# Taking the narrow weight blocks of a two-layer decoder eight or four at a time instead of two

## The chip, the cores and the metric

The kernel runs on one core of a Trainium2 chip. The metric is the device time of one execution in microseconds (us). A core has five engines that run side by side and wait for each other through semaphores: TensorE (PE, matrix products into PSUM; PEld is the part of it that loads the stationary operand), VectorE (DVE), ScalarE (ACT), GpSimd (POOL) and SyncE (SP, which here only issues transfers). Sixteen DMA engines move data between HBM and the core's memory.

## The reference, cut to what matters

A decoder trunk of two layers, width 2048, on 256 tokens, all in fp32. Both layers end in the same squared-ReLU MLP, which holds most of the weights.

```
def squared_relu_mlp(h, w1, w2):
    z = jax.nn.relu(h @ w1)          # w1: 2048 x 8192
    return (z * z) @ w2              # w2: 8192 x 2048

for i in range(2):
    if i == 1:
        sk1, sk2, sv = shared_kv(x, kv_norm, w_kv, k_norm, cos, sin)
    u = rms_norm(x, mix_norm[i]) @ w_in[i]          # 2048 x 2048
    # layer 0: causal pooling mixer; layer 1: differential attention; both: memory attention
    x = x + concat([token_out, mem_out]) @ w_out[i] # 2048 x 2048
    x = x + squared_relu_mlp(rms_norm(x, ffn_norm[i]), w_ff1[i], w_ff2[i])
```

## The kernel before

**Numbers in two parts.** Each fp32 operand is held as a high part, rounded to the TensorE format fp32r, and a low part, the rest. A product is high times high, plus high times low, plus low times high. The activations of 128 features lie side by side as 256 columns of high parts and 256 columns of low parts, 512 columns in all.

**Narrow and wide.** The weights come in blocks of 128 x 128, laid out in HBM in the order of use, eight to a row of 128 x 1024. In a *narrow* product one block is the stationary operand and the activations stream past it. The block's high part meets all 512 columns; its low part meets only the 256 high columns and adds to the second half of the same PSUM bank. So a block costs one matmul of 512 columns and one of 256, each with its own weight load. Narrow products are:

- the up projection `w_ff1` of each MLP: `up_tile` calls `narrow` (L940) with 16 blocks, 64 tiles a layer;
- the rest of the down projection `w_ff2`: `down_tile` calls `narrow` with 20 blocks, 8 tiles a layer;
- the output projection `w_out` and the pooling part of `w_in`: `a_part` (L512), whose tiles have 16 blocks, some of them in pieces.

In a *wide* product the activations are stationary and four blocks (a quad, 512 columns of weights) stream past: `wide_step`, `b_tile`, and the slab jobs of the MLP (`run`, L1038 to L1040), which work off most of `w_ff2` by a scheme of seven products in place of eight. A third form, `c_tile` (L533 to L538) and `group_w` (L1345 to L1347), uses a block with three matmuls of 256 columns.

**Pairs.** Both narrow loops take two blocks at a time: two high matmuls, then two low ones (L522 and L524 in `a_part`, L947 and L949 in `narrow`). After every four blocks they call `tick()`.

**The feed.** Class `Feed` hands out the blocks. For each job ACT rounds a piece of a loaded row into the high ring (L178) and DVE subtracts to make the low part (L181). In the MLP's up projection a job is a whole row, eight blocks (`rows_whole`, kept in `plan.whole`); elsewhere it is a quad. `fill` prepares three jobs ahead, when the first block of a job is asked for; `used` gives the slots back at the end of a row or quad. The ring has six slots of a quad, with two more in the MLP (`slot`).

**Deferred work.** `at(d, fn)` puts a piece of work d ticks ahead; `tick` runs what is due. The ReLU, squares and splits of the MLP (`convert`, at up to 10 ticks behind a tile) and the collecting of finished banks are placed so.

**Order.** The code is written in one order; a scheduler under it then orders each engine's instructions by its own estimate of times, so that small changes in the code can swap neighbours on ACT, DVE and SP. In the MLP up tiles and slab jobs alternate by `ffn_plan`: as a rule an up tile, then two or four slab jobs. While the seven slab banks are open, all up tiles share one PSUM bank, `x_bank`: ACT copies it out (L961) before the next tile may start.

Of the kernel before, what the change touches and what calls it, by code (L numbers as in the profile page):

```python
# [19 lines left out]
T = 256  # L20
# [85 lines left out]
class Feed:  # L106
# [151 lines left out]
    def block(self, what):  # L258
# [2 lines left out]
        s = slice(self.pos % 4 * P, self.pos % 4 * P + P)  # L261
        return hi[:, s], lo[:, s]

    def used(self, n=1):
        self.pos += n
        if self.dry:
            self.plan.npos = self.pos
        elif (self.pos - 1) // 8 in self.plan.whole:
            if self.pos % 8 == 0:
                self.free(("R", self.pos // 8 - 1))  # L270
        elif self.pos % 4 == 0:
            self.free(("N", self.pos // 4 - 1))
# [91 lines left out]
def program(ctx, tc, plan, dry, xT, memT, par, lam, cst, wst, yT):  # L364
    nc = tc.nc
# [9 lines left out]
    feed = Feed(tc, wst, wp, tp, plan, dry)  # L375
# [10 lines left out]
    def tick():  # L386
        now[0] += 1
        for _, fn in sorted(pend.pop(now[0], []), key=lambda r: r[0]):
            fn()
# [9 lines left out]
    def bk(tag, name, shape=(P, 512)):  # L399
        return pp.tile(list(shape), F32, tag=tag, bufs=1, name=name)  # L400
# [3 lines left out]
    def mmt(name):  # L404
        turnm[0] += 1
        return bk(f"m{(turnm[0] - 1) % 3}", name)
# [7 lines left out]
    def in_halves(name):  # L414
        return Halves(
            [sp.tile([P, NK // 2, 512], F32R, tag=f"S2{i}", name=f"{name}{i}") for i in "ab"]
        )
# [94 lines left out]
    def a_part(ps, w, l, n, ks, xs, first=True, last=True):  # L512
        ks = list(ks)
        i = 0
        while i < len(ks):
            two = []
            for k in ks[i : i + (1 if feed.pos % 2 else 2)]:
                two.append((i, k, *feed.block((w, l, k, n, 1))))
                feed.used()
                i += 1  # L520
            for j, k, hi, lo in two:
                nc.tensor.matmul(ps, hi, xs[:, k, :], start=first and j == 0, stop=False)  # L522
            for j, k, hi, lo in two:
                nc.tensor.matmul(  # L524
                    ps[:, T : 2 * T], lo, xs[:, k, 0:T], start=False,
                    stop=last and j == len(ks) - 1,
                )
            if feed.pos % 4 == 0:
                tick()

    def c_tile(ps, w, l, n, ks, xs):
# [306 lines left out]
    def ffn(l, xs, tag, done):  # L838
# [99 lines left out]
                at(d, fn)  # L938

        def narrow(ps, w, n, ks, src):  # L940
            for j in range(0, len(ks), 2):
                two = []
                for k in ks[j : j + 2]:
                    two.append((k, *feed.block((w, l, k, n, 1))))
                    feed.used()
                for k, hi, lo in two:
                    nc.tensor.matmul(ps, hi, src(k), start=k == ks[0], stop=False)  # L947
                for k, hi, lo in two:
                    nc.tensor.matmul(  # L949
                        ps[:, T : 2 * T], lo, src(k)[:, 0:T], start=False, stop=k == ks[-1]  # L950
                    )
                if j % 4 == 2:
                    tick()

        def up_tile(j, ps):
            narrow(ps, "w_ff1", j, list(range(NK)), lambda k: xs[:, k, :])
            if j == 1:
                r2c.append(columns("x")[1])
                r2.append(rstd_from("x"))
                nc.scalar.activation(r2[0], r2[0], AF.Square)  # L960
            nc.scalar.copy(pairs[j // 2 % 3][:, 512 * (j % 2) : 512 * (j % 2) + 512], ps)  # L961
            if j % 2:
                convert(j // 2, (1, 1, 2, 2, 3, 4, 5, 6) if j == 63 else STEPS)
# [7 lines left out]
        def down_tile(q, n, ps):  # L971
            ks = list(range(2 * NB, 4 * NK))
            if l == 1 and q == 3 and n == 7:
                narrow(ps, "w_ff2", n, ks[:-4], z)
                end = mmt("end")
                nc.scalar.copy(douts[downs[0] % 2], ps)
                add_down(n, douts[downs[0] % 2])
                for k in ks[-4:]:
                    hi, lo = feed.block(("w_ff2", l, k, n, 1))
                    zk = z(k)  # L980
                    nc.tensor.matmul(end[:, 0:T], hi, zk[:, 0:T], start=k == ks[-4], stop=False)
                    nc.tensor.matmul(end[:, 0:T], hi, zk[:, T : 2 * T], start=False, stop=False)
                    nc.tensor.matmul(end[:, 0:T], lo, zk[:, 0:T], start=False, stop=k == ks[-1])
                    feed.used()
                tick()
                for i in range(NB, 32):
                    left(i, "N")
                rest = douts[(downs[0] + 1) % 2][:, 0:T]
                nc.vector.tensor_mul(rest, end[:, 0:T], r2[0])
                nc.vector.tensor_add(resid[:, n, :], resid[:, n, :], rest)  # L990
                done(n)
                return
            narrow(ps, "w_ff2", n, ks, z)
            for i in range(NB, 32):
                left(i, "N")
# [206 lines left out]
    xs = in_halves("xs0")  # L1202
# [75 lines left out]
    ps = [mmt("mq0"), bk("o", "mq0")]  # L1278
# [28 lines left out]
    def group_u(g):  # L1307
        up = ups[g % 2]
        for c in range(3):
            ps = mmt("u")  # L1310
            a_part(ps, "w_in", 0, 3 * g + c, range(NK), xs)
            low = vt("u_c")
            nc.scalar.copy(low, ps[:, T : 2 * T])
            nc.vector.tensor_add(low, ps[:, 0:T], low)
            nc.vector.tensor_mul(up[:, c, 16:], low, x_r[0])
# [37 lines left out]
    def out_tiles(l, cat, lead, ks, fx, between):  # L1353

        first = [mmt("wo") for _ in range(3)]
        for i, part in enumerate(lead):
            for n in range(3):
                a_part(first[n], "w_out", l, n, part, cat, first=i == 0, last=False)
        between()
        for n in range(NK):  # L1360
            if n < 3:
                ps = first[n]
                a_part(ps, "w_out", l, n, ks, cat, first=False)
            else:
                ps = bk(f"n{n - 3}", "wo") if n < 5 else mmt("wo")
                a_part(ps, "w_out", l, n, sum(lead, []) + ks, cat)
            resid_add(ps, n)
            resid_done(n, [(fx, G_FFN + 16 * l)])
# [86 lines left out]
    def pair_of_banks(c, name):  # L1455
        if c % 2:
            return [bk(f"n{i}", name) for i in range(2)]
        return [mmt(name) for _ in range(2)]

    for c in range(3):  # L1460
        ps = pair_of_banks(c, "k1") if c else [mmt("k1"), bk("o", "k1")]
# [8 lines left out]
    for c in range(3):  # L1470
        ps = pair_of_banks(c + 1, "v1")
# [183 lines left out]
    for c in range(3):  # L1655
        ps = pair_of_banks(0, "q1")
# [4 lines left out]
        for i in range(2):  # L1661
            j = 2 * c + i
# [10 lines left out]
    for h in range(4):  # L1673
        ps = bk((ma, mb, mc, mb)[h], "mq1")
# [16 lines left out]
    for n, part in parts + [(n, range(NK)) for n in range(5, NK)]:  # L1691
        first = n not in opened
# [12 lines left out]
    down, _ = ffn(1, fx1, "S1", lambda n: nc.sync.dma_start(yT[:, n, :], resid[:, n, :]))  # L1705
# [84 lines left out]
```

## Time and profile before

| | |
|---|---|
| median of 3 runs | 2014.07 us (2012.58 to 2014.2) |
| the profiled execution's own time | 2016.58 us |
| its span | 2014.8 us |
| DVE busy | 1754.6 us (87%) |
| ACT busy | 1371.6 us (68%) |
| POOL busy | 163.3 us (8%) |
| HBM read, written | 425.61 MB, 12.58 MB |
| granted TensorE clock | 1.0 throughout |

The span runs from the first instruction to the last; 1.8 us of the execution lie around it. Busy times count a matmul from its start to its modelled end, and matmuls overlap, so PE's busy share does not say how fast it works; the starts in the timeline do. An engine's idle time counts only where it is waited for.

### The profile page before, as it was taken

Reading aid. Unit: us, or ns where it says so; the run is one execution under the profiler, and the core shown is the slowest. Engines: PE = TensorE matmul, PEld = TensorE weight load, DVE = VectorE, ACT = ScalarE, POOL = GpSimd, SP = SyncE. Lnnn points to the kernel's source line nnn. Section 1 sums busy time; section 2 is a strip of 40 time slices with the busy share of each in tenths; the row PEclk is TensorE's granted clock in tenths of the full one; section 3 lists DMA queues with packets and bytes.
Section 4 is the critical chain, followed back from the end, with each engine's and each line's share of the span. In section 5 each row is a group of like instructions: output and inputs, shape, how many; then the busy total and the mean of one; then the engine's idle time right before and its main releaser. Section 6 shows DMA issues by size and latency. Waiting matters only on the chain.

```text
span 2014.8 us, 30584 instructions
## 1 busy us (share of the span) xinstructions
PE 2003.7 (99%) x10636; PEld 1709.2 (85%) x10636; DVE 1754.6 (87%) x2665; ACT 1371.6 (68%) x2209; POOL 163.3 (8%) x191
## 2 busy tenths in 40 slices
PE   9999999999999999999999999999999999999999
PEld 7888888888888888888888889888888888888887
DVE  8888778999999999998775698878899999999987
ACT  7765467676666677667665698557676677677664
POOL 0001300000001110000000000320000000101000
PEclk9999999999999999999999999999999999999999
DMA  9566767777878888756656545666777877878775
GB/s 310 183 195 201 231 205 214 239 226 227 247 230 241 250 224 264 214 180 214 227 183 195 187 143 174 216 222 213 234 233 221 247 223 231 264 232 240 243 214 157
DMA packets 135370, 442.95 MB, mean 220 GB/s; under 512 B 15344, under 2 KB 18416, under 8 KB 135216
## 3 DMA queue, kind: packets, MB, share of 16 engines
q1 hardware_dynamic: 117216, 406.39, 60.4%
q0 software_dynamic: 17856, 34.61, 10.4%
q8 instruction: 83, 1.36, 0.3%
q14 instruction: 71, 0.58, 0.1%
q10 hardware_dynamic: 144, 0.01, 0.0%
HBM read 425.61 MB, written 12.58 MB: 217 GB/s over the span
## 4 chain that ended last, share of the span: by engine, by line
PE 55%; DVE 1%; DMA 1%; ACT 1%; issue 0%; POOL 0%; ACTq 0%; DVEq 0%; POOLq 0%
PE x_bank L947 13%; PE x_bank L949 6%; PE p L1038 5%; PE p L1040 5%; PE p L1039 5%; PE wo L522 3%; PE k L553 3%; PE v L553 3%; PE q L553 3%; PE ff L947 2%; PE wo L524 1%; PE mv L553 1%; PE mk L553 1%; PE ff L949 1%; DMA c_b<-part 1%; DVE lo_ring L181 1%
## 5 line engine op out<-in xcount | busy, mean ns | idle before, releaser
L181 DVE TENSOR_TENSOR lo_ring<-raw,hi_ring 128x512 fp32r<-128x512 f32 (+1 forms) x685 | 570.1, 847 | 128.4 <-ACT hi_ring L178 121.3
L178 ACT CAST hi_ring<-raw 128x512 fp32r<-128x512 f32 (+1 forms) x685 | 497.5, 741 | 231.4 <-PE wo L522 67.2
L181 DVE TENSOR_TENSOR lo_ring<-slab,hi_ring 128x1024 fp32r<-128x1024 f32 (+1 forms) x324 | 334.5, 1042 | 48.9 <-ACT hi_ring L178 47.3
L178 ACT CAST hi_ring<-slab 128x1024 fp32r<-128x1024 f32 (+1 forms) x324 | 293.5, 907 | 112.9 <-DVE slab L212 56.9
L149 POOL DMA_DIRECT2D slab<-in_w x108 | 93.6, 867 | 1575.9 <-DVE lo_ring L181 468.8
L947 PE MATMUL x_bank<-fx,hi_ring 128*128 128x512 f32 x664 | 209.2, 395 | 0.0
L522 PE MATMUL wo<-cat,hi_ring 128*128 128x512 f32 x512 | 161.6, 396 | 0.0
L178 ACT CAST slot<-slab 128x1024 fp32r<-128x1024 f32 x108 | 113.4, 1050 | 68.0 <-PE x_bank L947 62.8
L181 DVE TENSOR_TENSOR slot<-slab,slot 128x1024 fp32r<-128x1024 f32 x108 | 131.8, 1220 | 21.7 <-ACT slot L178 21.2
L949 PEld LDWEIGHTS x_bank<-fx,lo_ring 128*128 128x128 f32 x664 | 124.7, 188 | 29.4
L947 PE MATMUL x_bank<-fx0b,hi_ring 128*128 128x512 f32 x472 | 148.2, 395 | 0.0
L961 ACT COPY room<-x_bank 128x512 f32<-128x512 f32 x118 | 68.9, 584 | 99.2 <-PE x_bank L949 99.1
L212 DVE TENSOR_TENSOR slab<-slab,slab 128x1024 f32<-128x1024 f32 x108 | 131.6, 1218 | 0.4
L949 PE MATMUL x_bank<-fx,lo_ring 128*128 128x256 f32 x664 | 130.8, 278 | 0.0
L524 PEld LDWEIGHTS wo<-cat,lo_ring 128*128 128x128 f32 x512 | 96.0, 188 | 22.0
L949 PEld LDWEIGHTS x_bank<-fx0b,lo_ring 128*128 128x128 f32 x472 | 88.7, 188 | 21.0
L947 PEld LDWEIGHTS x_bank<-fx,hi_ring 128*128 128x128 f32 x664 | 103.0, 189 | 2.2
L524 PE MATMUL wo<-cat,lo_ring 128*128 128x256 f32 x512 | 101.7, 278 | 0.0
L178 ACT CAST slot<-raw 128x1024 fp32r<-128x1024 f32 (+1 forms) x76 | 74.1, 976 | 28.6 <-PE x_bank L947 21.9
L181 DVE TENSOR_TENSOR slot<-raw,slot 128x1024 fp32r<-128x1024 f32 (+1 forms) x76 | 85.9, 1132 | 8.0 <-ACT slot L178 7.9
L949 PE MATMUL x_bank<-fx0b,lo_ring 128*128 128x256 f32 x472 | 92.7, 278 | 0.0
L947 PE MATMUL x_bank<-fx0a,hi_ring 128*128 128x512 f32 x280 | 88.0, 395 | 0.0
(561 smaller groups left out, 4787.9 us busy)
## 6 DMA issues: line engine op xcount, KB each, us to landing
raw<-in_w SPq DMA_DIRECT2D x508, 512.0 KB, 4.5
slab<-in_w SPq DMA_DIRECT2D x216, 512.0 KB, 3.8
slab<-in_w POOLq DMA_DIRECT2D x108, 256.0 KB, 5.0
part<-room SPq DMA_DIRECT2D x6, 512.0 KB, 4.7
kept<-resida SPq DMA_DIRECT2D x4, 512.0 KB, 4.6
room<-part POOLq DMA_DIRECT2D x4, 512.0 KB, 8.6
resida<-kept SPq DMA_DIRECT2D x4, 512.0 KB, 7.5
memraw<-in_mem SPq DMA_DIRECT2D x4, 512.0 KB, 3.9
```

The lines of the kernel that those rows point to most:

```text
L149: self.nc.gpsimd.dma_start(t[:, 512:1024], self.wst[other, :, 512:1024], accum_op=ALU.add)
L178: cast = self.nc.scalar.copy(hi, src)
L181: self.nc.vector.tensor_sub(lo, src, hi.bitcast(F32))
L212: add(two, t.unsqueeze(1).to_broadcast([P, 2, 512]), two)
L522: nc.tensor.matmul(ps, hi, xs[:, k, :], start=first and j == 0, stop=False)
L524: nc.tensor.matmul(ps[:, T : 2 * T], lo, xs[:, k, 0:T], start=False, stop=last and j == len(ks) - 1,)
L553: nc.tensor.matmul(ps[t], a, b, start=i == 0 and j == 0, stop=i == NK - 1 and j == 2)
L947: nc.tensor.matmul(ps, hi, src(k), start=k == ks[0], stop=False)
L949: nc.tensor.matmul(ps[:, T : 2 * T], lo, src(k)[:, 0:T], start=False, stop=k == ks[-1])
L1038: nc.tensor.matmul(ps, al, hi[:, s], start=i == begin, stop=False)
L1039: nc.tensor.matmul(ps, ah, hi[:, s], start=False, stop=False)
L1040: nc.tensor.matmul(ps, ah, lo[:, s], start=False, stop=i == end - 1)
```

## The change

Both narrow loops now ask the feed for a group of blocks (`blocks`): as many as are left of the row where whole rows are split (at most eight), as many as are left of the quad elsewhere (at most four). They issue the high matmuls of the group, then its low matmuls. Only then is the group marked as used (`done`), and `tick()` is called once for each quad that it completed, so twice in a row after a group of eight.

```
+    def blocks(self, whats):
+
+        row = 8 if self.dry and self.rows_whole or self.pos // 8 in self.plan.whole else 4
+        some = []
+        for what in whats[: row - self.pos % row]:
+            some.append(self.block(what))
+            self.pos += 1
+        self.pos -= len(some)
+        return some
+
+    def done(self, n):
+        quads = 0
+        for _ in range(n):
+            self.used()
+            quads += self.pos % 4 == 0
+        return quads
...
         while i < len(ks):
-            two = []
-            for k in ks[i : i + (1 if feed.pos % 2 else 2)]:
-                two.append((i, k, *feed.block((w, l, k, n, 1))))
-                feed.used()
-                i += 1
-            for j, k, hi, lo in two:
-                nc.tensor.matmul(ps, hi, xs[:, k, :], start=first and j == 0, stop=False)
-            for j, k, hi, lo in two:
+            some = feed.blocks([(w, l, k, n, 1) for k in ks[i:]])
+            for j, (hi, lo) in enumerate(some, i):
+                nc.tensor.matmul(ps, hi, xs[:, ks[j], :], start=first and j == 0, stop=False)
+            for j, (hi, lo) in enumerate(some, i):
                 nc.tensor.matmul(
-                    ps[:, T : 2 * T], lo, xs[:, k, 0:T], start=False,
+                    ps[:, T : 2 * T], lo, xs[:, ks[j], 0:T], start=False,
                     stop=last and j == len(ks) - 1,
                 )
-            if feed.pos % 4 == 0:
+            i += len(some)
+            for _ in range(feed.done(len(some))):
                 tick()
...
         def narrow(ps, w, n, ks, src):
-            for j in range(0, len(ks), 2):
-                two = []
-                for k in ks[j : j + 2]:
-                    two.append((k, *feed.block((w, l, k, n, 1))))
-                    feed.used()
-                for k, hi, lo in two:
+            j = 0
+            while j < len(ks):
+                some = feed.blocks([(w, l, k, n, 1) for k in ks[j:]])
+                for k, (hi, lo) in zip(ks[j:], some):
                     nc.tensor.matmul(ps, hi, src(k), start=k == ks[0], stop=False)
-                for k, hi, lo in two:
+                for k, (hi, lo) in zip(ks[j:], some):
                     nc.tensor.matmul(
                         ps[:, T : 2 * T], lo, src(k)[:, 0:T], start=False, stop=k == ks[-1]
                     )
-                if j % 4 == 2:
+                j += len(some)
+                for _ in range(feed.done(len(some))):
                     tick()
```

Three places show what this does to the order of instructions. In the rows `L` is the line of the respective kernel (L947 and L949 become L959 and L961, L522 and L524 become L535 and L537, L1038 to L1040 become L1051 to L1053, L915, L930 and L961 on ACT become L929, L944 and L974).

On PE, inside the MLP of layer 0, the end of one up tile and the slab jobs behind it, before (`fx0a` and `fx0b` are the normed activations, `x_bank` the tile's PSUM bank, `p` the slab banks):

```order
L949 MATMUL x_bank<-fx0a,lo_ring 128x256 x2
L947 MATMUL x_bank<-fx0b,hi_ring 128x512 x2
L949 MATMUL x_bank<-fx0b,lo_ring 128x256 x2
L947 MATMUL x_bank<-fx0b,hi_ring 128x512 x2
L949 MATMUL x_bank<-fx0b,lo_ring 128x256 x2
L947 MATMUL x_bank<-fx0b,hi_ring 128x512 x2
L949 MATMUL x_bank<-fx0b,lo_ring 128x256 x2
L947 MATMUL x_bank<-fx0b,hi_ring 128x512 x2
L949 MATMUL x_bank<-fx0b,lo_ring 128x256 x2
L1038 MATMUL p_2899<-slot_2626,za_2623 128x512
```

And now, a whole up tile between two stretches of slab jobs:

```order
L1053 MATMUL p_2902<-lo_ring,za_2623 128x512
L959 MATMUL x_bank<-fx0a,hi_ring 128x512 x8
L961 MATMUL x_bank<-fx0a,lo_ring 128x256 x8
L959 MATMUL x_bank<-fx0b,hi_ring 128x512 x8
L961 MATMUL x_bank<-fx0b,lo_ring 128x256 x8
L1051 MATMUL p_2896<-slot_2626,za_2623 128x512
```

The same 32 matmuls stand there, with two turns from high to low in place of eight.

On PE, in the output projection of layer 0, from one tile of 16 blocks (`wo_1997`) into the next, before:

```order
L522 MATMUL wo_1997<-cat0_566,hi_ring_76 128x512 x2
L524 MATMUL wo_1997<-cat0_566,lo_ring_77 128x256 x2
L522 MATMUL wo_2049<-cat0_566,hi_ring_76 128x512 x2
L524 MATMUL wo_2049<-cat0_566,lo_ring_77 128x256 x2
L522 MATMUL wo_2049<-cat0_566,hi_ring_76 128x512 x2
```

And now, the last eight blocks of that tile and the first high parts of the next:

```order
L535 MATMUL wo_1997<-cat0_566,hi_ring_76 128x512 x4
L537 MATMUL wo_1997<-cat0_566,lo_ring_77 128x256 x4
L535 MATMUL wo_1997<-cat0_566,hi_ring_76 128x512 x4
L537 MATMUL wo_1997<-cat0_566,lo_ring_77 128x256 x4
L535 MATMUL wo_2049<-cat0_566,hi_ring_76 128x512 x4
```

Groups of four stand in place of pairs, without a pause between tiles.

On ACT, in the MLP of layer 0, around the copy that empties `x_bank`, before (`raw` are rows of narrow weights, `slab` those of the slab jobs, `room` and `za` the MLP's values):

```order
L178 CAST hi_ring<-raw_3071 128x1024
L178 CAST hi_ring<-slab_2974 128x512
L915 CAST za_2623<-room_2625 128x2x256
L178 CAST hi_ring<-raw_3094 128x1024
L930 CAST za_2623<-room_2625 128x512
L961 COPY room_2625<-x_bank 128x512
```

And now:

```order
L178 CAST hi_ring<-raw_3071 128x1024
L178 CAST hi_ring<-slab_2974 128x512
L929 CAST za_2623<-room_2625 128x2x256
L944 CAST za_2623<-room_2625 128x512
L178 CAST hi_ring<-raw_3094 128x1024
L974 COPY room_2625<-x_bank 128x512
```

The rounding of a weight row has moved behind the rounding of the sums, next to the copy; the rest is in its old order.

## The prediction

> **What bounds the kernel now.** I read the engine totals of the page first, then PE's waits, then PE's timeline.
>
> ```profile
> span 2014.8 us, 30584 instructions
> PE 2003.7 (99%) x10636; PEld 1709.2 (85%) x10636; DVE 1754.6 (87%) x2665; ACT 1371.6 (68%) x2209; POOL 163.3 (8%) x191
> PE mk L553 <- ACT hi_ring L178: 2.0, 3, 1.0
> PE ct L1116 <- ACT room L961: 1.8, 1, 1.8
> PE warm L465 <- DVE ones_d L456: 1.1, 1, 1.1
> PE p L1040 <- DVE slot L181: 0.6, 1, 0.6
> PE p L1040 <- DVE lo_ring L181: 0.4, 1, 0.4
> PE mv L553 <- DVE lo_ring L181: 0.2, 1, 0.2
> ```
>
> PE is busy for 99% of the span, and all that it waits for adds up to 6.1 us (2.0 + 1.8 + 1.1 + 0.6 + 0.4 + 0.2), none of it in front of a narrow matmul. So neither the splitting of weights nor the transfers bound the narrow stages; the pace at which PE starts matmuls does. The mean durations do not give that pace, since matmuls overlap (395 ns for a high one and 278 ns for a low one in the page's groups). Starts do.
>
> **The pace of the two kinds.** First the two extremes: a stretch of 512-column matmuls only (slab jobs), and one of 256-column matmuls only (`c_tile`, a weight load before each).
>
> ```profile
> 456.32 0.39 PE L1040 MATMUL p<-lo_ring,zb 128*128 128x512 f32 x1
> 459.04 0.39 PE L1040 MATMUL p<-lo_ring,zb 128*128 128x512 f32 x1
> ...
> 1194.10 0.28 PE L535 MATMUL mq<-x_mx,hi_ring 128*128 128x256 f32 x1
> 1194.33 0.28 PE L537 MATMUL mq<-x_mx,lo_ring 128*128 128x256 f32 x1
> 1194.57 0.28 PE L536 MATMUL mq<-x_mx,hi_ring 128*128 128x256 f32 x1
> 1195.05 0.28 PE L537 MATMUL mq<-x_mx,lo_ring 128*128 128x256 f32 x1
> 1196.97 0.39 PE L1617 MATMUL do<-big,att 128*128 128x128 f32 x2
> ```
>
> From 456.32 to 459.04 there are 12 starts: 0.2267 us for a 512-column matmul in a run. From 1194.33 to 1196.97 there are 22: 0.120 us for a 256-column one. The run begins faster, after 512-column ones: two take 0.23, four 0.47, eight 0.95 us.
>
> Then the pairs, in the longest undisturbed stretch, the output projection of layer 0; the row of the windows view counts its high matmuls.
>
> ```profile
> 180.65 0.63 PE L522 MATMUL wo<-cat,hi_ring 128*128 128x512 f32 x2
> 251.71 0.63 PE L522 MATMUL wo<-cat,hi_ring 128*128 128x512 f32 x2
> ...
> 180.60:251.70 71.10, 64.06 (x204) 31.09 (x205) 1.00 0.69 225
> ```
>
> 204 high matmuls are 102 pairs in 71.06 us, 0.6967 us a pair. At the pace of pure runs a pair would take 2 x 0.2267 + 2 x 0.120 = 0.6933 us. So the mixing costs only 3.3 ns a pair. The narrow loops hold 2 x 64 x 16 blocks of `w_ff1`, 320 of `w_ff2`, 512 of `w_out` and 192 of `w_in`: 3072 blocks, 1536 pairs. **All that grouping could ever save in pace is 1536 x 3.3 ns = 5.1 us**, and only if a turn from low to high cost the same however long the run before it.
>
> **What a turn costs.** The rows say that it does not. Here are two stretches of slab jobs behind the low matmuls of an up tile, with the tile before one of them.
>
> ```profile
> 298.93 0.62 PE L947 MATMUL x_bank<-fx0a,hi_ring 128*128 128x512 f32 x2
> 301.71 0.62 PE L947 MATMUL x_bank<-fx0b,hi_ring 128*128 128x512 f32 x2
> 304.50 0.40 PE L1038 MATMUL p<-slot,za 128*128 128x512 f32 x1
> 307.23 0.61 PE L947 MATMUL x_bank<-fx0a,hi_ring 128*128 128x512 f32 x2
> 312.79 0.40 PE L1038 MATMUL p<-slot,za 128*128 128x512 f32 x1
> ...
> 454.25 0.40 PE L949 MATMUL x_bank<-fx0b,lo_ring 128*128 128x256 f32 x2
> 454.48 0.40 PE L1038 MATMUL p<-slot,zb 128*128 128x512 f32 x1
> 455.41 0.39 PE L1039 MATMUL p<-slot,zb 128*128 128x512 f32 x1
> 458.13 0.39 PE L1039 MATMUL p<-hi_ring,zb 128*128 128x512 f32 x1
> 459.27 0.62 PE L947 MATMUL x_bank<-fx0a,slot 128*128 128x512 f32 x2
> ```
>
> Behind 304.50, 12 matmuls take 2.73 us, 0.01 over 12 x 0.2267. Behind 454.48, 21 take 4.79 us, 0.03 over 21 x 0.2267. The first eight of these take 1.84 us (to 456.32), the next eight 1.81 (to 458.13). So there are a cheap and a dear turn to high. Pairs alternate between them: in a pair the low run ends before it has settled to 0.120, and the next high run pays little or much by turns. The dear turn comes where the last low matmul started about 0.12 us before the next start, which is how the matmuls of a long low run follow each other. **I choose to charge every turn behind four or eight low matmuls as dear, 0.03 us.** This is the step on which the forecast rests; it is taken from runs of two, since no run of eight low parts is followed by a run of eight high ones in the trace.
>
> **The change part by part.** PE issues the same matmuls and weight loads; only their order within a group changes.
>
> 1. *Up tiles, 128 of them.* Before, a tile takes 5.57 us (298.93 to 304.50) or 5.56 (307.23 to 312.79) and the turn behind it 0.01 more: 5.575. Now it is 1.81 + 0.95 for the first eight blocks, behind wide matmuls, 1.84 + 0.95 for the second, and the dear turn behind it, 0.03: 5.58. The hundredths leave the difference open between -0.01 and +0.03; by the long average, four pairs take 4 x 0.6967 = 2.787 and a group of eight in the middle 1.84 + 0.95 = 2.79. I take +0.013 us a tile, near the middle: 128 x 0.013 = **+1.7 us** (-1.3 to +3.8).
> 2. *Groups of four*, in `a_part` and the down tiles: (512 + 192 + 320) / 4 = 256. Each takes 0.93 (454.48 to 455.41) + 0.47 = 1.40 us, where two pairs take 1.393: +0.007, 256 x 0.007 = **+1.8 us**. The other end is four of each kind at the pace of pure runs, 1.387, so -1.6 us; some turns may be cheap here, since four high matmuls do not end the aftermath that lasts for eight, and the trace does not show a low run that starts there.
> 3. *Waits.* A low part is now first needed 8 x 0.2267 = 1.81 us after the group's first start instead of 0.46. That can only take away waits for DVE; the two at L1040 (0.6 + 0.4 us) are in slab jobs, which DVE reaches a little earlier. I take **-0.5 us**, half of these (-1.0 to 0). Activations of a group's last blocks are needed earlier, by 3 x 0.6967 + 0.23 - 7 x 0.2267 = 0.73 us at most in an up tile; PE waits for no activation of a narrow tile now, so this costs nothing unless the cover is thinner than 0.73 us.
> 4. *Moved work.* High slots are free earlier (the eighth high part starts 0.73 us earlier), low slots of the first half of a row later (its fourth low part starts 1.81 + 3 x 0.12 = 2.17 us into the group instead of 1.28, 0.9 us). ACT and DVE work three jobs ahead, over 5 us, so both stay hidden. The tick in the middle of a group of eight comes four blocks later. On ACT and DVE the order hardly changes, as the rows on ACT show. SP's and POOL's transfers keep their count; some neighbours swap.
>
> Sum: 1.7 + 1.8 - 0.5 = +3.0 us on the profiled execution's 2016.58, that is 2019.6. That execution lies 2.5 us above the median of the runs, 2014.07, so the forecast for the median is **2017.1 us**, 0.15% up. A measurement of this kernel can tell about 0.2% (4 us) from no change.
>
> [...]
>
> **Rivals.**
>
> - *A turn has one price.* Then fewer turns cost less in proportion: three of four go in the 1024 pairs of the up tiles, one of two in the other 512: 1024 x 3.3 x 3/4 + 512 x 3.3 / 2 = 3.4 us saved, 2010.7. For it: 102 pairs average to one steady number. Against it: 0.01 and 0.03 behind otherwise equal tiles.
> - *Order does not matter to pace.* A matmul's time would hang on its own columns alone, and nothing waits: 2014.1. For it: the whole effect of mixing is 3.3 ns in 697. The dear and the cheap turn speak against it, by little. [...]
> - *Slower: the copy of `x_bank` comes late.* All up tiles between slab jobs share one bank.
>
> ```profile
> 296.83 0.62 ACT L930 CAST za<-room 128x512 fp32r<-128x512 f32 x1 [0.31 <-DVE room L926]
> 297.35 0.58 ACT L961 COPY room<-x_bank 128x512 f32<-128x512 f32 x1
> 298.23 1.05 ACT L178 CAST slot<-slab 128x1024 fp32r<-128x1024 f32 x1 [0.29 <-PE p L1039]
> ```
>
> The copy ends at 297.93, 1.0 us before the next tile starts (298.93). The scheduler now puts the rounding of a row, 1.05 us, right ahead of it. Where that row is not ready sooner, the copy ends 0.05 us too late; on all 118 tiles that the page counts for this copy +6 us, 2020. It decides once the copy slips by over 1.0 us behind stretches of only nine slab matmuls. Against it: the rounding only changes places with work that stood there, and the subtraction it waited for (L926, 0.31) now comes earlier.
>
> **How the numbers follow.** Dear turns (+3.0; the ends of its terms add up to -3.9 and +5.6): 0.45. One price: 0.22. No effect: 0.13. Late copy: 0.15. Something unseen: 0.05. Against the bound of 4 us: of the first, 0.17 lies above it; of the second, half lies beyond 4 us on the other side, since low runs may start faster than I read; the third is no change; the fourth is slower but for 0.01. That makes faster 0.13, same 0.53, slower 0.34. The first alone spans 2010 to 2020; with the late copy and what the runs scatter the range is 2010 to 2021.5.
>
> **What would show it.** In the timeline of the changed kernel: eight high matmuls in 1.84 us behind eight low ones (1.81 or 1.82 would be a cheap turn and bring the first rival), eight low in 0.95, four and four in 1.40; an up tile with its turn at 5.58 or more; no row with PE behind `room` in the waits (the third rival), and none behind `cat` or `fx`. Waits of PE that add up to some us more than 6.1 would make the forecast wrong whatever the turns cost.

## The result and the profile after

The changed kernel takes 2017.74 us (median of 20 runs, 2015.6 to 2019.52), the kernel before 2014.66 beside it (20 runs, 2012.58 to 2016.95): **ratio 1.0016, 95% interval 1.0009 to 1.0023**, some 3.2 us slower. A second set of runs gave 1.0016 again (1.0007 to 1.0024). Every ratio in this text is to runs of the kernel before on the same chip. The forecast was 2017.1, +0.15%. The number is right; the sum behind it is not. Two of its four terms were right, and the two others are each wrong by over 2 us, in opposite directions. That these two errors cancel is luck. The rest of this text shows how the four terms came apart.

The page of the changed kernel first, then all of PE's waits:

```profile
span 2015.9 us, 30594 instructions
PE 2003.7 (99%) x10636; PEld 1719.8 (85%) x10636; DVE 1753.4 (87%) x2665; ACT 1372.1 (68%) x2209; POOL 161.7 (8%) x191
...
PE ct L1129 <- ACT c_b L1118: 2.2, 1, 2.2
PE mv L567 <- DVE lo_ring L181: 1.6, 1, 1.6
PE mk L567 <- ACT hi_ring L178: 1.5, 1, 1.5
PE warm L482 <- DVE ones_d L473: 1.1, 1, 1.1
PE p L1051 <- ACT hi_ring L178: 0.7, 2, 0.4
PE p L1053 <- DVE lo_ring L181: 0.4, 1, 0.4
PE p L1053 <- DVE slot L181: 0.2, 1, 0.2
PE mk L567 <- DVE lo_ring L181: 0.2, 1, 0.2
```

Busy time of PE is the same to the tenth, which says nothing here, since PE's records overlap. The waits add up to 7.9 us instead of 6.1. No wait of PE for `room` stands at `x_bank`: the copy of the bank did not come late, and that rival is out. New are `ct` behind `c_b`, 2.2 us, and two waits of `p` for `hi_ring`; the wait of `mv` for `lo_ring` has grown from 0.2 to 1.6. Gone is `ct` behind `room`, 1.8 us, which the single profiled execution before had held. That execution took 2016.58 us and the one after 2017.66, 1.1 us apart, so the two traces show a third of what the medians do; regions have to be compared over several kernels.

Then PE's timeline: one up tile with the slab jobs behind it (the nine rows of slab matmuls between 330.20 and 332.26 are left out), and the first and last start of 49 groups of four in the output projection.

```profile
324.64 1.98 PE L959 MATMUL x_bank<-fx0a,hi_ring 128*128 128x512 f32 x8
326.45 1.11 PE L961 MATMUL x_bank<-fx0a,lo_ring 128*128 128x256 f32 x8
327.40 2.00 PE L959 MATMUL x_bank<-fx0b,hi_ring 128*128 128x512 f32 x8
329.25 1.12 PE L961 MATMUL x_bank<-fx0b,lo_ring 128*128 128x256 f32 x8
330.20 0.40 PE L1051 MATMUL p<-slot,za 128*128 128x512 f32 x1
...
332.26 1.98 PE L959 MATMUL x_bank<-fx0a,hi_ring 128*128 128x512 f32 x8
...
182.19 1.09 PE L535 MATMUL wo<-cat,hi_ring 128*128 128x512 f32 x4
...
250.94 0.40 PE L535 MATMUL wo<-cat,hi_ring 128*128 128x512 f32 x1
```

Eight high matmuls behind slab matmuls take 1.81 us, eight behind low ones 1.85 (1.841 in the mean of 134 such runs), eight low ones 0.95. The tile takes 5.56, and the nine slab matmuls behind it 2.06 where 9 x 0.2267 is 2.04: 5.58 with its turn. All of this is as forecast. A group of four takes 68.75 / 49 = 1.403 us against 2 x 0.6967 = 1.393 for two pairs, +9.7 ns where the forecast had 7.

### The profile page after: what moved, and what is told of

The parts are those of the page before. It is cut to its first block, busy times and chain, and to the rows that moved or that the text cites. A ratio compares the mean times of both kernels' runs of the same rounds, so it can differ in the third digit from the quotient of the medians.

```text
span 2015.9 us, 30594 instructions
## 1 busy us (share of the span) xinstructions
PE 2003.7 (99%) x10636; PEld 1719.8 (85%) x10636; DVE 1753.4 (87%) x2665; ACT 1372.1 (68%) x2209; POOL 161.7 (8%) x191
## 4 chain that ended last, share of the span: by engine, by line
PE 96%; DVE 1%; DMA 1%; ACT 0%; issue 0%; SPq 0%; POOL 0%; ACTq 0%; DVEq 0%; POOLq 0%
PE x_bank L959 23%; PE x_bank L961 12%; PE p L1051 8%; PE p L1053 8%; PE p L1052 8%; PE wo L535 6%; PE wo L537 3%; PE q L567 3%; PE k L567 3%; PE v L567 3%; PE ff L959 3%; PE u L535 2%; PE mv L567 2%; PE mk L567 2%; PE ff L961 1%; PE u L537 1%
## 5 line engine op out<-in xcount | busy, mean ns | idle before, releaser
L974 ACT COPY room<-x_bank 128x512 f32<-128x512 f32 x118 | 69.0, 584 | 149.5 <-PE x_bank L961 149.5
L959 PE MATMUL x_bank<-fx,hi_ring 128*128 128x512 f32 x664 | 166.4, 392 | 0.0
L535 PE MATMUL wo<-cat,hi_ring 128*128 128x512 f32 x512 | 142.0, 395 | 0.0
L959 PEld LDWEIGHTS x_bank<-fx,hi_ring 128*128 128x128 f32 x664 | 120.8, 189 | 23.0 <-ACT room L974 0.5
L959 PE MATMUL x_bank<-fx0b,hi_ring 128*128 128x512 f32 x472 | 118.2, 392 | 0.0
L959 PEld LDWEIGHTS x_bank<-fx0b,hi_ring 128*128 128x128 f32 x472 | 84.9, 189 | 15.2
L535 PEld LDWEIGHTS wo<-cat,hi_ring 128*128 128x128 f32 x512 | 87.1, 189 | 11.6 <-DVE cat L426 0.4
L961 PEld LDWEIGHTS x_bank<-fx,lo_ring 128*128 128x128 f32 x664 | 90.6, 190 | 6.5
L961 PE MATMUL x_bank<-fx,lo_ring 128*128 128x256 f32 x664 | 92.6, 282 | 0.0
L537 PEld LDWEIGHTS wo<-cat,lo_ring 128*128 128x128 f32 x512 | 79.7, 189 | 11.3
L537 PE MATMUL wo<-cat,lo_ring 128*128 128x256 f32 x512 | 83.5, 281 | 0.0
L1051 PE MATMUL p<-hi_ring,zb 128*128 128x512 f32 x210 | 82.8, 394 | 0.4 <-ACT hi_ring L178 0.4
```

The costliest lines, as they stand in the source:

```text
L535: nc.tensor.matmul(ps, hi, xs[:, ks[j], :], start=first and j == 0, stop=False)
L537: nc.tensor.matmul(ps[:, T : 2 * T], lo, xs[:, ks[j], 0:T], start=False, stop=last and j == len(ks) - 1,)
L961: nc.tensor.matmul(ps[:, T : 2 * T], lo, src(k)[:, 0:T], start=False, stop=k == ks[-1])
L1051: nc.tensor.matmul(ps, al, hi[:, s], start=i == begin, stop=False)
```

## Experiments

### Turns by themselves

PE alone, with nothing to wait for: twelve stretches of 48 blocks, each in another grouping, between runs of 14 512-column matmuls. It leaves out the whole decoder.

```
SECTIONS = ((1,), (2,), (3,), (4,), (6,), (8,), (16,), (1, 2), (1, 3), (2, 3), (2, 4), (1, 1, 2))
```

> PE alone, nothing to wait for: 12 stretches of 48 narrow blocks, in groups of 1, 2, 3, 4, 6, 8, 16 and in mixtures (1,2), (1,3), (2,3), (2,4), (1,1,2), each between 14 wide matmuls of 512 columns; it leaves out the whole decoder. At the pace of pure runs a stretch takes 48 x (0.2267 + 0.120) = 16.64 us. Theory 'dear turn' (a turn to high costs more once the low run before it has settled): over that, groups of 8 cost 6 x 20 ns = 0.12 us, groups of 16 0.06, groups of 4 about 12 x 9 = 0.11, pairs 24 x 3.3 = 0.08; so 4 and 8 take longer than 2. Rival 'one price' (every turn 3.3 ns): pairs 0.08, fours 0.04, eights 0.02, sixteens 0.01. Rival 'crowding' (the extra time comes from the traffic of DVE, ACT and DMA beside PE): no extra at all here, since nothing else runs.

The timeline of this kernel, at a granted clock of 1.00, for pairs, fours, eights and sixteens: the start of a stretch, and of the 512-column run behind it.

```profile
36.30 0.62 PE L52 MATMUL narrow<-xs,hi 128*128 128x512 f32 x2
...
53.01 3.35 PE L41 MATMUL wide<-hi,xs 128*128 128x512 f32 x14
...
76.16 1.07 PE L52 MATMUL narrow<-xs,hi 128*128 128x512 f32 x4
...
92.98 3.38 PE L41 MATMUL wide<-hi,xs 128*128 128x512 f32 x14
...
116.17 1.98 PE L52 MATMUL narrow<-xs,hi 128*128 128x512 f32 x8
...
132.90 3.36 PE L41 MATMUL wide<-hi,xs 128*128 128x512 f32 x14
136.10 3.79 PE L52 MATMUL narrow<-xs,hi 128*128 128x512 f32 x16
...
152.78 3.36 PE L41 MATMUL wide<-hi,xs 128*128 128x512 f32 x14
```

Pairs take 16.71 us, fours 16.82, eights 16.73, sixteens 16.68. The same from the starts in nanoseconds, with the aftermath in the 512-column run counted in, and less 48 x 226.67 + 48 x 120:

```
grouping           ones  pairs  threes  fours  sixes  eights  sixteens
excess, ns          319     80     160    219    160     120        60
turns back to high   48     24      16     12      8       6         3
ns a turn           6.7    3.3    10.0   18.3   20.0    20.0      20.0
```

**In equal groups, from two low matmuls on, the price of a turn grows with the run before it, and stays at 20 ns from six on.** Pairs, eights and sixteens cost what was expected, fours twice the 0.11 us. Nothing else runs here, so the extra time does not come from the traffic of other engines, the rival called crowding. Fewer turns do not cost less in proportion, so the rival with one price is out. Of the equal groups, pairs are the cheapest below sixteens.

The mixed stretches show that the low run before a turn does not set its price alone. Twos and fours in turn cost 93 ns over pure pace, where the prices above would give 173; twos and threes in turn cost 239, where they would give 130. So the table holds for a row of equal groups, which is what the narrow loops issue.

### One part of the change at a time

The grouping is one expression in `blocks`. In order: eights in up tiles with pairs elsewhere; fours outside the up tiles with pairs in them; fours in the projections alone; fours in the down tiles alone; fours everywhere; ones everywhere.

```
-        row = 8 if self.dry and self.rows_whole or self.pos // 8 in self.plan.whole else 4
+        row = 8 if self.dry and self.rows_whole or self.pos // 8 in self.plan.whole else 2
...
+        row = 2 if self.dry and self.rows_whole or self.pos // 8 in self.plan.whole else 4
...
+        row = 4 if whats[0][0] in ("w_in", "w_out") else 2
...
+        row = 4 if whats[0][0] == "w_ff2" else 2
...
+        row = 4
...
+        row = 1
```

> Groups of eight in the up tiles, pairs as before elsewhere. Dear turn: the up tiles' share of the loss, 128 x 13 ns = +1.7 us, ratio 1.0008. One price: 1024 x 3.3 x 3/4 = -2.6 us, ratio 0.9987.

> The change itself once more, on the chip of the three runs beside it, so that they can be compared with it directly. By the dear turn its narrow tiles cost +1.7 us in the up tiles and +1.8 to +3.0 us in the groups of four, less the small waits of the up phases that went; a ratio of 1.0010 to 1.0022 to the kernel before. By one price of a turn it would be 0.9983, by an order that doesn't matter 1.0000.

> The other half of the change alone: pairs in the up tiles as before, groups of four in the projections and the down tiles (256 groups). Dear turn: +7 ns a group as the prediction had it gives +1.8 us, 1.0009; the 11.6 ns a group that the matmuls by themselves showed (4.58 for four against two pairs of 3.3 ns a pair, with 48 blocks at 219 against 80 ns of excess) give +3.0 us, 1.0015. One price of a turn: -0.85 us, 0.9996. Order doesn't matter: 1.0000. The small waits of the up phases stay as before in this kernel, if it is the eights that took them away.

> Groups of four in the projections alone (w_in and w_out, 704 blocks, 176 groups), pairs in up and down tiles. Theory A, the 6.2 us of the run with fours outside the up tiles is pace: 176 of 256 groups carry two thirds of it, +4 us, 1.002. Theory B, pace is only the 9 to 11.6 ns a group that the starts and the matmuls by themselves showed, and the rest are waits in the down phases: here +1.6 to +2.0 us, 1.0008 to 1.0010, with no wait of ct behind c_b.

> Groups of four in the down tiles alone (w_ff2, 320 blocks, 80 groups), pairs elsewhere. Theory A: a third of 6.2 us, +2 us, 1.001, without new waits. Theory B: 80 groups at 9 to 11.6 ns are +0.7 to +0.9 us of pace, and a new wait comes with them: ct behind c_b of 1 to 2.5 us near the end of the first layer's down phase, since the chain of subtractions ahead of the read-back of the partial sums ends later against the transposes; with a longer wait for slot in the second layer's down phase that makes +2 to +4 us, 1.0010 to 1.0020. The two theories are told apart by that wait in the trace more than by the time.

> Groups of four everywhere, in the up tiles too. Dear turn: a middle group of four is 1.402 us in the changed kernel against 1.393 for two pairs, and an up tile with its turn 5.614 against 5.573 us, so 128 x 0.040 + 2 = about +7 us, ratio 1.0036, worse than the change. One price: half of all turns go, 1536 x 3.3 / 2 = -2.5 us, ratio 0.9987.

> Groups of one everywhere: a high matmul, then its low one. One price: twice the turns, 1536 x 3.3 = +5.1 us, ratio 1.0025. Dear turn: open, because a low run of one never settles; the few single blocks in the trace of before take 693 ns (233, 117, 231, 112) or 712 ns (234, 117, 241, 120) for two, against 697 for a pair, so between -6 and +23 us, by which of the two patterns a long alternation falls into.

```
                            us       ratio to before, 95%
eights in up tiles alone    2012.55  0.9996 (0.9987 to 1.0005)
the change again            2016.30  1.0016 (1.0007 to 1.0024)
fours outside the up tiles  2020.01  1.0031 (1.0020 to 1.0043)
fours in projections alone  2016.25  1.0008 (0.9999 to 1.0017)
fours in down tiles alone   2018.70  1.0020 (1.0011 to 1.0028)
fours everywhere            2021.34  1.0036 (1.0022 to 1.0050)
ones everywhere             2029.25  1.0075 (1.0062 to 1.0088)
```

Fours outside the up tiles cost 6.2 us where the highest expectation was 3.0, a miss; that is why the two runs that split them were made. Fours in the projections cost 1.6 us for 176 groups, 9 ns a group, which is pace. Fours in the down tiles cost 4.0 us for 80 groups: 0.8 at that pace, so 3.2 are something else, and their trace shows waits. Eights alone cost nothing, although their pace is worse. That is a miss for the 1.0008 of the dear turn; the 0.9987 of one price lies at the end of the interval, and the turns by themselves speak against it.

The parts do not add up well: eights (-0.8 us) and fours outside the up tiles (+6.2) make +5.4 us, where the change itself costs 3.2. The intervals are wide enough for both, so this stays open.

Where the time lies shows in the length of each phase, from the start of its first matmul to that of the next phase's first, in one profiled execution of each kernel (us; order, sixteens and low parts last are the experiments below):

```
                     up, both layers  down 0  down 1  out projections
before                       1202.81   76.90   78.68   190.62
order of eights, pairs       1200.79   76.91   78.21   190.60
fours in projections         1201.44   77.27   77.58   191.80
fours in down tiles          1201.45   80.80   77.84   190.60
fours outside up tiles       1201.43   79.39   79.77   191.76
eights alone                 1200.83   77.47   78.19   190.60
the change                   1199.74   79.85   78.04   191.76
the change again             1199.72   82.15   77.94   191.75
sixteens                     1207.17   78.08   77.15   190.62
fours everywhere             1205.28   78.81   79.25   192.05
ones everywhere              1212.76   77.28   78.16   191.62
low parts last, pairs        1205.58   77.46   77.65   190.62
low parts last, eights       1200.00   77.61   77.55   190.63
```

The output projections repeat to 0.05 us, and their 128 groups of four cost 1.15 us, 9 ns each, in every kernel that has them but the one with fours everywhere (1.4 us). Layer 0's down phase takes 76.9 to 78.1 us with pairs or ones and 78.8 to 82.2 with fours, whatever the up tiles have. The longest, 82.15 in the change again, holds something else too: behind its wait at `ct` the granted clock was 0.54 from 922.6 to 926.0 us, where the other traces have 1.00 in this phase. An estimate from these numbers is 1.6 us lost to that clock.

The up phases take 1201.3 with pairs (mean of the four kernels with pairs in the up tiles and slab jobs as before, without the 1.8 us behind `room`) and 1200.1 with eights (mean of the three with slab jobs as before): eights gain about 1.2 us there, though their pace costs 1.7. Single traces overlap (1200.79 with pairs, 1200.83 with eights), so the 1.2 is rough.

**Down tiles.** What is new in their phase is one wait. It stands in the waits of the run with fours in the down tiles alone:

```profile
PE ct L1129 <- ACT c_b L1118: 2.5, 1, 2.5
```

It is in all the kernels with fours in the down tiles (2.2 and 2.5 in the two traces of the change, 1.1 in the one with fours outside the up tiles, 1.2 with fours everywhere) and in none of those with pairs there. The place in the kernel before, from PE's, ACT's and POOL's timelines and the transfers of that stretch (the last two rows give the us from issue to landing):

```profile
919.66 0.27 PE L1116 MATMUL ct<-const,c_b 128*128 128x128 f32 x1
918.76 0.72 ACT L1105 ACTIVATE c_b<-c_b,d_x 128x512 f32<-128x512 f32 x1 [2.44 <-DMA c_b<-part]
907.05 0.93 POOL L1088 DMA_DIRECT2D c_b<-part  x1
c_a<-part POOLq DMA_DIRECT2D x1, 512.0 KB, 6.1
c_b<-part POOLq DMA_DIRECT2D x1, 512.0 KB, 11.7
```

and in the changed kernel:

```profile
919.15 0.27 PE L1129 MATMUL ct<-const,c_a 128*128 128x128 f32 x1
921.60 0.33 PE L1129 MATMUL ct<-const,c_b 128*128 128x128 f32 x1 [2.18 <-ACT c_b L1118]
920.82 0.72 ACT L1118 ACTIVATE c_b<-c_b,d_x 128x512 f32<-128x512 f32 x1 [3.17 <-DMA c_b<-part]
907.57 0.88 POOL L1101 DMA_DIRECT2D c_b<-part  x1 [0.24 <-issue]
c_a<-part POOLq DMA_DIRECT2D x1, 512.0 KB, 10.5
c_b<-part POOLq DMA_DIRECT2D x1, 512.0 KB, 13.2
```

PE transposes `c_b` once ACT has scaled it, and ACT waits until the parked sums have been added to it by a transfer. Before, scaling ended at 918.76 + 0.72 = 919.48 and PE came at 919.66: **a cover of 0.18 us, with no wait to show for it.** After, the transfer is issued 0.5 us later, takes 1.5 longer, and PE comes about 0.4 earlier. Those 2.4 less the cover are the wait of 2.2. Why the same 512 KB take longer (`c_a` 10.5 instead of 6.1) was not tried. It goes with the distance of the two issues: in the six traces where `c_b` is issued 0.85 to 0.86 us behind `c_a`, `c_a` takes 6.0 to 6.3, and in the seven where 1.12 or 1.13 lie between, 8.1 to 10.8.

Right behind this phase a second wait has grown. The first products of `mv` wait 1.5 to 1.6 us for `lo_ring` in four of the five kernels with fours in the down tiles, and 0.2 in the change again and in all kernels without them. Its cause was not tried. The stretch from there to the next output projection is no longer for it, 301.30 us against 301.28 before.

### Why eights lose no time: order or need

Bookkeeping of eights (ticks and release of slots once per eight blocks) with matmuls in pairs, and pairs elsewhere:

```
+        row = 8 if self.dry and self.rows_whole or self.pos // 8 in self.plan.whole else 2
...
+                for i in range(0, len(some), 2):
+                    two = list(zip(ks[j + i : j + i + 2], some[i : i + 2]))
```

> Pairs everywhere as the kernel before has them, but in the up tiles the bookkeeping goes as in the change: ticks and the release of ring slots come once per eight blocks. It tells why the small waits between up tiles and slab jobs went in the run with eights in the up tiles alone. Theory A, the ticks come later and put the other engines' work in another order: the waits go here too, the pace is that of the kernel before, about -1.5 to -2.5 us, ratio 0.9988 to 0.9993. Theory B, the waits go because low parts are needed 1.35 us later in a group of eight: here they stay, ratio 1.0000, and the stalls between steady up tiles number about 19 of 104 as in the kernel before.

2013.65 us, 1.0002 (0.9993 to 1.0010). This is what theory B expected; the time alone just touches the upper end of theory A. To see the small waits one has to look at the weight loads, which stand ahead of the matmuls and wait in their place. The waits of PEld at slab jobs, before:

```profile
PEld p L1040 <- DVE lo_ring L181: 4.5, 16, 0.8
PEld p L1038 <- ACT hi_ring L178: 3.2, 10, 0.5
PEld p L1038 <- ACT slot L178: 1.9, 4, 0.5
PEld p L1040 <- DVE slot L181: 1.3, 2, 1.0
```

and after:

```profile
PEld p L1051 <- ACT hi_ring L178: 3.2, 9, 0.8
PEld p L1053 <- DVE lo_ring L181: 2.3, 5, 0.8
PEld p L1053 <- DVE slot L181: 1.3, 3, 0.7
```

Waits for `lo_ring` fall from 16 to 5 (7 with eights alone); with the order of eights and the pace of pairs they stay at 16, 4.8 us. So the later ticks and releases do not take these waits away, and the grouping of the matmuls does. That they go because a low part is needed later is theory B's reason; it fits, but the run with low parts last, below, shows that it is no general rule. One of them in the kernel before, on the timelines of PE, PEld and DVE:

```profile
629.61 0.39 PE L1039 MATMUL p<-hi_ring,za 128*128 128x512 f32 x1
629.84 0.39 PE L1038 MATMUL p<-hi_ring,za 128*128 128x512 f32 x1
630.17 0.50 PE L1040 MATMUL p<-lo_ring,za 128*128 128x512 f32 x1
630.51 0.40 PE L1039 MATMUL p<-hi_ring,za 128*128 128x512 f32 x1
630.75 0.39 PE L1040 MATMUL p<-lo_ring,za 128*128 128x512 f32 x1
...
630.17 0.19 PEld L1040 LDWEIGHTS p<-lo_ring,za 128*128 128x128 f32 x1 [0.37 <-DVE lo_ring L181]
...
628.90 1.22 DVE L181 TENSOR_TENSOR lo_ring<-slab,hi_ring 128x1024 fp32r<-128x1024 f32 x1
```

DVE ends at 630.12, the load starts at 630.17, and the starts of the matmuls around it lie 0.33 and 0.34 us apart in place of 0.23. This late part costs 0.22 us, and PE's own waits list none of it.

The starts of the up phases can be counted through, from the first matmul of an up tile to the first of the next, slab jobs included; 118 such stretches a kernel hold nothing else. The count is over the pace of pure runs:

```
                            stretches over by 90 ns or more   all 118, us over
before                                   32                        11.6
order of eights, pairs                   36                        11.0
the change                               22                        10.1
eights alone                             22                        10.5
```

An up tile that runs in one piece, with the five slab matmuls behind it, lies 26 to 27 ns over pure pace with pairs (75 of 101 such tiles) and 39 to 40 with eights (104 of 106): the 13 ns of the forecast. Take this pace off the last column and the waits are 8.4 and 7.8 us with pairs, 5.3 and 5.8 with eights, so about 2.6 us less.

### Longer groups, and low parts later in the slab jobs

Sixteens: up tiles as 16 high and 16 low parts. Where a tile begins at some places in the row, the expression still splits it in two eights; 86 runs of sixteen low matmuls are in the trace, so about a third of the tiles are eights.

```
+        row = 16 if self.dry and self.rows_whole or self.pos // 8 in self.plan.whole else 2
+        if row == 16:
+            row += self.pos % row
```

> Whole up tiles as sixteen high parts and then sixteen low parts, pairs elsewhere. Dear turn (20 ns for each settled round trip): one turn in a tile in place of the two of eights, 20 ns against 40 ns, 128 tiles, -2.6 us against the kernel with eights in the up tiles alone (0.9996), so about 0.9983; against the kernel before -0.85 us of pace and the small waits besides. One price of a turn: three quarters of the way again, 0.9983 too, but then eights would have been faster than pairs. Rival: sixteen high slots are held at once and ACT can't fill the next ones ahead, so PE comes to wait for hi_ring or for room and the run is slower than with eights, 1.001 or more; it shows as waits of PE behind ACT.

2019.53 us, 1.0033 (1.0021 to 1.0046): as slow as the rival said, where the dear turn had 0.9983. Undisturbed tiles of sixteen do cost 20 ns over pure pace, as expected. The waits are those of the weight loads, for ACT as the rival said and more still for DVE. That both come from slots held too long is argued, not shown. PEld's waits at slab jobs:

```profile
PEld p L1055 <- DVE lo_ring L181: 14.1, 56, 0.5
PEld p L1053 <- ACT hi_ring L178: 10.2, 38, 0.3
```

PE's own waits in this kernel hold no row of `p` at all, though its up phases are 6 us longer than those of the pairs.

The last two runs: in slab jobs of two sides the four matmuls with high parts first and the two with low parts behind them, once with pairs everywhere, once with eights in the up tiles.

```
-                    nc.tensor.matmul(ps, ah, lo[:, s], start=False, stop=i == end - 1)
+                for s, ah, al, ps in some:
+                    nc.tensor.matmul(ps, ah, lo[:, s], start=False, stop=i == end - 1)
```

> Pairs everywhere as in the kernel before; in a slab job with two sides the four matmuls with high parts come first and the two with low parts last. If the small waits of the up phases are for low parts that DVE delivers late (theory B of the run with the order of eights and the pace of pairs), the weight loads' waits for lo_ring at slab jobs fall from 16 (4.5 us) to under 8, and the time by 1 to 2 us: 0.9990 to 0.9995. Rival: DVE and ACT work in lockstep and a low part that comes late makes the next high part late too; then the waits for hi_ring and slot grow by as much and the time stays, 1.0000.

> Eights in the up tiles alone, pairs elsewhere, and low parts last in slab jobs: the candidate for a version that beats both. Pace of the up tiles +1.7 us (39.9 against 26.6 ns a tile) as with eights alone, waits for lo_ring at slab jobs from 7 to about 3. If both ways of needing the low part later add up: 0.9988 to 0.9994. If eights have already taken what there is to take: the ratio of eights alone again, 0.9996.

With pairs 2020.15 us, 1.0024 (1.0015 to 1.0033), a miss for both theories. Waits for `lo_ring` rose, those for `hi_ring` fell to 4 (1.7 us). PEld's waits, and one place on PE's timeline:

```profile
PEld p L1053 <- DVE lo_ring L181: 12.7, 37, 0.7
...
405.84 0.40 PE L1051 MATMUL p<-hi_ring,za 128*128 128x512 f32 x1
406.07 0.40 PE L959 MATMUL x_bank<-fx0a,hi_ring 128*128 128x512 f32 x1
406.39 0.72 PE L1053 MATMUL p<-lo_ring,za 128*128 128x512 f32 x2
406.95 0.40 PE L959 MATMUL x_bank<-fx0a,hi_ring 128*128 128x512 f32 x1
```

The order now has the two low matmuls of the last job behind the first matmul of the next up tile, and they still wait. So needing a low part later did not bring it in time here; why, these runs leave open. With eights 2013.70 us, 0.9994 (0.9985 to 1.0003): waits for `lo_ring` at slab jobs fall to 2 (0.6 us), but the time is that of eights alone, the second expectation. No version here beats it by more than the runs scatter.

## Why the number was right, step by step

1. *Up tiles, +1.7 us: right.* The choice on which the forecast rested, that every turn behind four or eight low matmuls is dear, holds for the groups that the change makes: eight behind eight take 1.841 us, and the 20 ns show by themselves. The tile's 13 ns are 40 against 27: 128 x 13 = 1.7.
2. *Groups of four, +1.8 us: right in kind, a little small.* 9 ns in place of 7, measured in the two output projections; the run with fours in the projections agrees, with a wide interval: 256 x 9 = 2.3.
3. *Waits, -0.5 us: mis-sized.* The forecast took half of the two waits that PE's list shows at slab jobs. The weight loads' list holds 16 waits for `lo_ring` there, 4.5 us, and the one shown above cost PE 0.2 us. Up phases are 1.2 us shorter although pace adds 1.7, so the waits are about **-2.9 us**; the count of the starts gives -2.6, and the time of eights alone (-0.8, less 1.7) -2.5. In that are two new ones for `hi_ring` (0.7 us by PE's list); without them it would be more.
4. *Moved work, nothing: this is the step that failed.* The text said of SP's and POOL's transfers that "some neighbours swap" and named only the three jobs by which ACT and DVE run ahead as cover. One transfer had 0.18 us of cover: **+2.2 to +2.5 us** in the change's two traces, all of it from fours in the down tiles. The prediction's own sign, waits of PE well above 6.1 us, showed less than that: they came to 7.9, because the 1.8 us behind `room` stood in the trace of before alone.

Sum: 1.7 + 2.3 - 2.9 + 2.3 = +3.4 us, where the medians say 3.2 (1.8 to 4.6) and the forecast 3.0. With -2.6 for step 3 it is 3.7. The errors of steps 3 and 4 are -2.4 (or -2.1) and +2.3. Nothing in the prediction ties the one to the other, so the sum came true by luck; steps 1 and 2 came true by their reason.

The rivals: one price for a turn fell with the turns by themselves, and with ones everywhere, which it put at 1.0025 and which came at 1.0075. That order does not matter to pace fell too: PE alone, with nothing to wait for, needs 16.71 us in pairs and 16.82 in fours. In the decoder, grouping alone moved the time from 0.9996 to 1.0075, waits included. The late copy of `x_bank` did not happen. But the slower side came by the same kind of mechanism, a thin cover behind work that moved, at another place.

## What to carry to other kernels

Read the waits of the weight loads beside PE's own, since small waits of matmuls stand there and the one shown here cost PE 0.2 us that its own list does not show. Before pricing moved work at nothing, list for the last stage of each phase how long ahead of its use each result is ready, above all those that come by a transfer; 0.18 us was the one that mattered. And a forecast that comes true is not yet a theory that holds: only the parts, taken one at a time, showed that two of its terms were wrong.

## What the runs showed of the hardware

- In a row of equal groups, a change from 256-column back to 512-column matmuls costs 3.3 ns behind two, 10 behind three, 18.3 behind four and 20 behind six, eight or sixteen (PE alone, granted clock 1.00). Ones cost 6.7, twice as much per turn as pairs. In mixed groups the prices differ: twos and fours in turn cost 93 ns in 16 turns.
- At the place shown, a weight load that comes late for one matmul shifts two starts: 0.33 and 0.34 us in place of 0.23, 0.22 us in all, where the load's own wait reads 0.37.
- The same read-back of 512 KB took 6.0 to 6.3 us from issue to landing in the traces where the next one was issued 0.85 us behind it, and 8.1 to 10.8 where that was 1.12. Why was not tried.
- Behind a wait of PE of 2.5 us, one trace has a granted clock of 0.54 for 3.4 us; the other traces with such a wait, 1.1 to 2.5 us long, keep 1.00.
